# A hybrid decoder step on one NeuronCore: a slot of its own for the last norm's rows, column sums by transposes, and w_o begun row by row

## The chip, the cores and the metric

The kernel runs on one core of a Trainium2 chip. The time is device microseconds of one execution. TensorE (PE in the profile) multiplies matrices, VectorE (DVE), ScalarE (ACT) and GpSimd (POOL) work element by element, and DMA queues on SyncE (SP), ACT and POOL move data. TensorE writes only into PSUM, eight banks of 128 x 512 floats; DVE and ACT read PSUM. Each engine takes its instructions in a fixed order, and an instruction that waits holds up all behind it on its engine or queue.

## The reference, cut to what matters

One layer for a prompt of 2048 tokens and 32 sample tokens (8 sequences of 4), model width 1024, in fp32:

```python
h = rmsnorm(x, n1);  z = h @ w_in
y_a = (rmsnorm(hgrn(z)) * silu(hg)) @ w_up_a      # recurrent branch
y_b = sliding_window_attention(z) @ w_up_b
m = sigmoid(ga) * y_a + sigmoid(gb) * y_b
x = x + m @ w_o
h2 = rmsnorm(x, n2)
x = x + square(relu(h2 @ w_ff1)) @ w_ff2
y = rmsnorm(x, normf_w)
```

where `rmsnorm(x, w) = x * rsqrt(mean(x*x, -1) + 1e-6) * w`. The outputs are y, the new key and value windows and the new recurrent states.

## The kernel before, in words

**Layout and precision.** Activations stand transposed: the 1024 features lie in eight rows of 128 partitions (k = 0 to 7), the tokens along the free axis. Every fp32 product is made of three matmuls of split operands (high x high, high x low, low x high): `split_out` copies to the high part on ACT and subtracts on DVE to get the low part. So each weight block costs a DMA, an ACT cast and a DVE subtraction. Weight tiles come from one ring, `wtile`, of 12 buffers of 128 x 1024.

**Stages.** The 2080 tokens are four blocks b0 to b3 of 512 (b3 holds the 32 sample tokens too, 544 in all, worked on in segments of 288 and 256). Two blocks make a half: half 0 is b0 and b1, half 1 is b2 and b3. Each block runs projections, recurrence, attention, the gates, and then w_o: eight output rows j, two to a weight unit, each a sum over eight rows of m (L1150 to L1163). In half 1 the projections are done for both blocks at once by a Strassen scheme (z). After b3 follow, for each half, FF1 and FF2, both by a Strassen scheme: FF1 by `strassen_T`, whose units first do their products with A11 and A12 and reach S1 to S4 and A22 later; FF2 in seven steps (`steps`), each a product over 16 blocks in four groups g. Steps one to six add into y (`evac`, L1301); y's rows j 0 to 3 of the first token part are whole after step five, all but the second part's rows 0 to 3 after step six, the rest in step seven, which goes by pairs jp of columns with four weight blocks each.

**Norms.** Each norm needs the mean of squares over the features, which lie across partitions. `Norm.add` squares a row on ACT and sums it into `acc` on POOL (L231). `rstd_row` (L200) sums over the partitions with matmuls against a column of 1/1024 (L207, tiles n_), adds epsilon on DVE (L209), raises to -1/2 on POOL (L210), and spreads the result over all partitions by transposes (L215, tiles rb_), copied out by ACT (L216). `Norm.scale` (L237) then multiplies on DVE. The first norm (L428) squares all eight rows and lets the matmuls sum them too.

**Work beside w_o.** During w_o the list `todo` runs pieces of the next work, `per` of them after each j: in b0 the norm of b1's input (tiles xr, na_h), in b1 the two norms of half 1 (zh, na_z; scaled rows are stored to DRAM, hraw, and the first half's are split into hT, which the next projection reads), in b2 a reload, in b3 `ff_sums`, FF1's sums of h2. The norm of w_o's own result (n2, tiles na_fb) is ended later, among the next block's projections (`late`).

**The last norm.** `Fin` (L1270) holds one token part of y: `add(j)` loads the residual row x1 into a `wtile` (on SP), adds it, squares into another `wtile`, and sums on POOL; `end` is the norm, `out(j)` scales and stores. Both parts are handled within step seven, their pieces again in a list `todo`, two after each group.

**What sets the order.** The code gives only priorities. A planner simulates the program with its own estimates of durations and puts on each engine, in turn, the ready instruction that comes first in the code; buffers are given out in the same pass. So moving code moves instructions only as far as that plan lets them, and the plan's estimates can be off.

## Time and profile before

| what | value |
|---|---|
| runs shown | 2982.37, 2985.49, 2986.84 us |
| median | 2985.49 us |
| profiled execution, own time | 2984.1 us |
| its span, first to last instruction | 2982.3 us |
| mean granted clock of TensorE | 0.973 |
| DMA queue of SP and ACT issues (q1) | 334.41 MB, 35.8% of 16 engines' time |
| DMA queue of POOL issues (q0) | 131.41 MB, 12.0% |

Spans and durations in the profile are of one execution. The profile's answers give, for a group of instructions, busy time and the mean duration of one, then the idle time of the engine just before them and what ended it. PE's waits are idle time that the trace puts down to the last semaphore to come. A matmul's recorded duration overlaps with the next one's, so the cost of a matmul is read from a dense stretch and not from its own record.

### The profile page before, as it was taken

What the parts mean: (1) busy time and instruction counts of PE and PEld (TensorE: products, weight loads), DVE (VectorE), ACT (ScalarE), POOL (GpSimd) and SP (SyncE); (2) the same over time, 40 slices, a digit from 0 to 9 for tenths busy, and PEclk for the clock granted to TensorE, in tenths of its full rate; (3) what the DMA queues carried; (4) which work ended last, traced back from release to release, by engine and by line L of the source; (5) the groups of instructions that cost most, each with busy time, mean ns of one, the idle gap of its engine ahead of it and who ended that gap; (6) DMA issues with size and microseconds to landing.
All of it is one profiled execution on the core that took longest, in us unless ns stands there. A gap on an engine that the chain in (4) does not pass through costs nothing.

```text
span 2982.3 us, 50304 instructions
## 1 busy us (share of the span) xinstructions
PE 2823.5 (95%) x20169; PEld 2461.4 (83%) x20169; DVE 1720.7 (58%) x2742; ACT 1131.4 (38%) x2128; POOL 556.0 (19%) x825
## 2 busy tenths in 40 slices
PE   8999999999899999999998999999987999999995
PEld 6778787787799968777897788778866999999994
DVE  3474444754765357436667877654556776644454
ACT  3442334423444444234334333444423333344331
POOL 0100321002510101320133222110023333300002
PEclk9999999999899999999999999999988999999997
DMA  4227642277553423423367544785546444555553
GB/s 136 78 74 251 202 130 67 63 252 229 183 190 101 147 85 119 154 81 101 106 216 236 175 155 156 247 279 197 188 158 199 150 156 142 182 193 190 179 174 123
DMA packets 342970, 480.31 MB, mean 161 GB/s; under 512 B 22208, under 2 KB 223760, under 8 KB 342720
## 3 DMA queue, kind: packets, MB, share of 16 engines
q1 hardware_dynamic: 292080, 334.41, 35.8%
q0 software_dynamic: 40288, 131.41, 12.0%
q10 hardware_dynamic: 10368, 11.28, 1.1%
q8 instruction: 158, 2.59, 0.4%
q14 instruction: 76, 0.62, 0.1%
HBM read 346.20 MB, written 131.83 MB: 160 GB/s over the span
## 4 chain that ended last, share of the span: by engine, by line
PE 76%; DMA 6%; issue 6%; POOL 5%; DVE 4%; ACT 2%; POOLq 0%; SPq 0%; ACTq 0%; DVEq 0%
PE f L1297 6%; PE f L1299 6%; PE f L1298 6%; PE fB_f L248 4%; PE fB_f L250 3%; PE fB_f L249 3%; PE fD_f L250 2%; PE fD_f L248 2%; PE fD_f L249 2%; PE fB_z L248 1%; PE fB_z L250 1%; PE fB_z L249 1%; PE ps_hgb L161 1%; PE ps_hgb L162 1%; PE ps_hgb L163 1%
## 5 line engine op out<-in xcount | busy, mean ns | idle before, releaser
L1297 PE MATMUL f<-f2S,hw2T 128*128 128x264 f32 (+1 forms) x576 | 185.0, 321 | 2.1 <-ACT hw2T L147 2.1
L1299 PE MATMUL f<-f2S,lw2T 128*128 128x264 f32 (+1 forms) x576 | 184.5, 320 | 0.3 <-DVE lw2T L148 0.3
L1298 PE MATMUL f<-f2S,hw2T 128*128 128x264 f32 (+1 forms) x576 | 184.6, 321 | 0.0
L231 POOL TENSOR_TENSOR na_y<-na_y,nq_y 128x512 f32<-128x512 f32 (+2 forms) x35 | 39.2, 1120 | 554.7 <-ACT nq_y L230 553.7
L148 DVE TENSOR_TENSOR lw2T<-lw2T,hw2T 128x1024 fp32r<-128x1024 f32 x64 | 78.1, 1227 | 99.5 <-ACT hw2T L147 98.7
L161 PE MATMUL wob<-m_b,h_wob 128*128 128x512 f32 (+2 forms) x320 | 115.9, 362 | 12.0 <-DVE x_b L1158 5.3
L248 PE MATMUL fB_f<-S,w1T_f 128*128 128x264 f32 (+1 forms) x384 | 123.5, 322 | 3.9 <-ACT c_f L310 3.2
L1297 PE MATMUL f<-f2A,h_w2B 128*128 128x264 f32 (+1 forms) x384 | 122.5, 319 | 0.6 <-ACT c_f L1202 0.6
L249 PE MATMUL fB_f<-S,w1T_f 128*128 128x264 f32 (+1 forms) x384 | 122.6, 320 | 0.0
L250 PE MATMUL fB_f<-S,w1T_f 128*128 128x264 f32 (+1 forms) x384 | 122.6, 320 | 0.0
L1298 PE MATMUL f<-f2A,h_w2B 128*128 128x264 f32 (+1 forms) x384 | 122.3, 319 | 0.0
L1299 PE MATMUL f<-f2A,l_w2B 128*128 128x264 f32 (+1 forms) x384 | 122.2, 318 | 0.0
L1297 PEld LDWEIGHTS f<-f2S,hw2T 128*128 128x128 f32 x576 | 109.0, 189 | 10.1 <-ACT hw2T L147 2.6
L162 PE MATMUL wob<-m_b,h_wob 128*128 128x512 f32 (+2 forms) x320 | 116.0, 362 | 1.1 <-DVE m_b L241 1.1
L147 ACT CAST hw2T<-lw2T 128x1024 fp32r<-128x1024 f32 x64 | 66.9, 1050 | 130.0 <-DMA lw2T<-w_T 129.6
L1299 PEld LDWEIGHTS f<-f2S,lw2T 128*128 128x128 f32 x576 | 108.7, 189 | 8.7 <-DVE lw2T L148 1.0
L163 PE MATMUL wob<-m_b,l_wob 128*128 128x512 f32 (+2 forms) x320 | 115.6, 362 | 0.0
L1298 PEld LDWEIGHTS f<-f2S,hw2T 128*128 128x128 f32 x576 | 109.1, 189 | 7.7
L148 DVE TENSOR_TENSOR f2S<-f2S 128x1024 fp32r<-128x1024 f32 (+1 forms) x64 | 79.1, 1240 | 46.9 <-ACT f2S L147 45.6
L240 ACT CAST w1T_f<-w1r_f 128x512 fp32r<-128x512 f32 x128 | 77.2, 619 | 72.3 <-DVE w1r_f L284 32.3
L241 DVE TENSOR_TENSOR l_w2B<-rw2B,h_w2B 128x1024 fp32r<-128x1024 f32 x48 | 58.7, 1223 | 75.5 <-ACT h_w2B L240 61.6
L241 DVE TENSOR_TENSOR w1T_f<-w1r_f,w1T_f 128x512 fp32r<-128x512 f32 x128 | 87.1, 687 | 25.9 <-ACT w1T_f L240 25.7
(794 smaller groups left out, 9486.3 us busy)
## 6 DMA issues: line engine op xcount, KB each, us to landing
w1r_f<-w_ff SPq DMA_DIRECT2D x64, 512.0 KB
lw2T<-w_T SPq DMA_DIRECT2D x64, 512.0 KB
rw2B<-w_ff SPq DMA_DIRECT2D x48, 512.0 KB
f2S<-u_S SPq DMA_DIRECT2D x32, 528.0 KB
ws<-w_ff SPq DMA_DIRECT2D x32, 512.0 KB
r_wob<-w_o SPq DMA_DIRECT2D x32, 512.0 KB
f2S<-u_S SPq DMA_DIRECT2D x32, 512.0 KB
u_S<-s_f POOLq DMA_DIRECT2D x96, 132.0 KB, 2.4
```

Of the source, the lines that this page charges most:

```text
L148: nc.vector.tensor_tensor(lo, F(lo), F(hi), ALU.subtract)
L161: nc.tensor.matmul(ps[:, 0:n], wh, rh, start=(k == 0), stop=False)
L162: nc.tensor.matmul(ps[:, 0:n], wh, rl, start=False, stop=False)
L163: nc.tensor.matmul(ps[:, 0:n], wl, rh, start=False, stop=(k == nk - 1))
L240: nc.scalar.copy(dh, src)
L241: nc.vector.tensor_tensor(dl, src, F(dh), ALU.subtract)
L248: nc.tensor.matmul(ps, wh, ah, start=(first and k == 0), stop=False, skip_group_check=not first)
L249: nc.tensor.matmul(ps, wh, al, start=False, stop=False, skip_group_check=not first)
L250: nc.tensor.matmul(ps, wl, ah, start=False, stop=(last and k == 3), skip_group_check=not first)
L1297: nc.tensor.matmul(ps, wh, ah, start=first, stop=False, skip_group_check=cont)
L1298: nc.tensor.matmul(ps, wh, al, start=False, stop=False, skip_group_check=cont)
L1299: nc.tensor.matmul(ps, wl, ah, start=False, stop=lastk, skip_group_check=cont)
```

## The change

- `rstd_row`: the accumulated squares are transposed by TensorE, 128 (or 88, 68) tokens at a time, into PSUM, and one DVE reduction per chunk sums over the features; one DVE instruction multiplies by 1/1024 and adds epsilon. The column `ones` is gone. The first norm's eight squared rows are summed on DVE.
- `Norm.add` takes an engine: DVE in b0, for the first of the two norms in b1, and for n2 in b3; POOL otherwise. Of the gate sums of m, row 6 goes to DVE as row 7 did.
- w_o: the first two output rows (n = 0) go row by row of m over both; PSUM tiles come from three rings in turn, not two; evictions and `todo` pieces come after each pair of output rows, one piece after each row. The lists are cut anew: in b0 and b1 a norm's end comes later in the list; in b1 the halves interleave, and hraw is stored two rows at a time on ACT's queue.
- `Fin`: residual rows and squares live in `xo`, slot 6 of the eight-row operand slots, in eight columns that are used in turn; `load` is apart from `add`; the first part's loads and its first four adds move into step six; the sums for the second part's rows 0 to 3 go to DVE, the others stay on POOL. In the last half one piece follows each group.

```diff
-    def rstd_row(dst, sqs, n, tmp, name):
+    def rstd_row(dst, sq, n, tmp, name):
-        ps = tp_ps(f"n_{name}")[0:w, 0:nt]
-        for i in range(nt):
-            for j, sq in enumerate(sqs):
-                nc.tensor.matmul(ps[:, i:i + 1], sq[:, i * w:(i + 1) * w], ones, start=(j == 0), stop=(j == len(sqs) - 1))
         rs = tmp("ns", f"rs_{name}")[0:w, 0:nt]
-        nc.vector.tensor_scalar(rs, ps, EPS, None, ALU.add)
+        for t0, ln in chunks_of(n):
+            ps = tp_ps(f"n_{name}_{t0}")[0:w].rearrange("p (c e) -> p c e", e=P)[:, 0:ln // w]
+            for i in range(ln // w):
+                nc.tensor.transpose(ps[:, i], sq[:, t0 + i * w:t0 + (i + 1) * w], ident)
+            nc.vector.tensor_reduce(rs[:, t0 // w:(t0 + ln) // w], ps, AX.X, ALU.add)
+        nc.vector.tensor_scalar(rs, rs, 1.0 / D, EPS, ALU.mult, ALU.add)
...
-        def add(u, x):
+        def add(u, x, eng=nc.gpsimd):
-                nc.gpsimd.tensor_tensor(u.acc, u.acc, q, ALU.add)
+                eng.tensor_tensor(u.acc, u.acc, q, ALU.add)
...
     for k in range(KD):
         nc.scalar.activation(sq0[:, k], x0[:, k], AF.Square)
+        if k:
+            tt(sq0[:, 0], sq0[:, 0], sq0[:, k], ALU.add)
...
-                (nc.vector if j == KD - 1 else nc.gpsimd).tensor_tensor(o, o, pb[:, j, t0:t0 + n], ALU.add)
+                (nc.vector if j >= KD - 2 else nc.gpsimd).tensor_tensor(o, o, pb[:, j, t0:t0 + n], ALU.add)
...
-            todo += [loads, lambda: [nn.add(xr[:, k]) for k in range(4)], lambda: [nn.add(xr[:, k]) for k in range(4, 8)] + [nn.end()]]
-            todo += [lambda k=k: fin1(k) for k in range(0, KD, 2)]
+            todo += [loads, lambda: [nn.add(xr[:, k], nc.vector) for k in range(4)], lambda: [nn.add(xr[:, k], nc.vector) for k in range(4, 8)],
+                     lambda: None, nn.end, lambda: [fin1(0), fin1(2)], lambda: [fin1(4), fin1(6)]]
...
-                        nc.gpsimd.dma_start(hraw[sb + 1][k * P:(k + 1) * P, o * Tn:(o + 1) * Tn], xr[:, k])
+                        if k % 2:
+                            nc.scalar.dma_start(kmaj(hraw[sb + 1], k - 1, 2, o * Tn, Tn), xr[:, k - 1:k + 1])
+            (ld0, sq0_, end0, fin0), (ld1, sq1_, end1, fin1_) = half
+            todo += [ld0, lambda: sq0_(0), lambda: [sq0_(4), ld1()], lambda: sq1_(0), lambda: [end0(), sq1_(4)], lambda: fin0(0),
+                     lambda: [fin0(4), end1()], lambda: [fin1_(0), fin1_(4)]]
...
+        rings = (sw_ps, mm_ps, hg_ps)
         for n in range(0, KD, 2):
             uo = [unit_rows(w_o, 4 * kh, 4, n * P, 2 * P, f"wo{B}{n}{kh}") for kh in range(2)]
+            ps = [[rings[j % 3](f"wo{B}{j}_{t0}")[:, 0:ln] for (t0, ln) in segs] for j in (n, n + 1)]
+            order = [(k, j, i) for j in range(2) for i in range(len(segs)) for k in range(KD)]
+            for k, j, i in (sorted(order) if n == 0 else order):
...
+                nc.tensor.matmul(p, wh, ah, start=(k == 0), stop=False)
+                nc.tensor.matmul(p, wh, al, start=False, stop=False)
+                nc.tensor.matmul(p, wl, ah, start=False, stop=(k == KD - 1))
+            for j in range(2):
...
+                n2.add(x1[:, n + j], nc.vector if last_b else nc.gpsimd)
+                if todo:
+                    todo.pop(0)()
...
+                def load(f, j):
                     c0 = f.o * Th + f.t0
-                    nc.sync.dma_start(x, x1d[sb][j * P:(j + 1) * P, c0:c0 + f.ln])
+                    nc.sync.dma_start(f.x(f.regs[j]), x1d[sb][j * P:(j + 1) * P, c0:c0 + f.ln])
+                def add(f, j, eng=nc.gpsimd):
+                    x = f.x(f.regs[j])
                     tt(f.y(j), f.y(j), x, ALU.add)
-                    f.n.add(f.y(j))
+                    nc.scalar.activation(x, f.y(j), AF.Square)
+                    if f.acc is None:
+                        f.acc = x
+                    else:
+                        eng.tensor_tensor(f.acc, f.acc, x, ALU.add)
...
+            f0 = Fin(0, 0, Th, {**{j: j for j in range(KD)}, "rb": 1})
+            f1 = [Fin(1, t0, ln, {4: 2, 5: 3, 6: 4, 7: 5, 0: 6, 1: 7, 2: 3, 3: 4, "rb": 5})
...
+                if si == 5:
+                    xo = raw8(6, Th, f"xo{sb}")
+                    todo += [lambda: [f0.load(j) for j in range(4)], lambda: [f0.load(j) for j in range(4, 8)],
+                             lambda: [f0.add(0), f0.add(1)], lambda: [f0.add(2), f0.add(3)]]
...
-                    if not last and si >= 1 and g % 2 and todo:
+                    if todo and (si == 5 or g % 2):
                         todo.pop(0)()
...
+            todo = [lambda j=j: f0.add(j) for j in range(4, KD)]
+            todo = todo[2:] + [each("load", 0, 1)] + todo[:2] + [each("load", 4, 5, 6, 7), none, f0.end, none]
+            outs = [lambda j=j: f0.out(j) for j in range(KD)]
+            todo += [each("add", 4), outs[0], each("add", 5), outs[1], each("add", 6), each("load", 2, 3), outs[2], each("add", 7)] + outs[3:]
...
-                            for _ in range(2):
+                            for _ in range(1 if last else 2):
...
-                        f.add(2 * jp + j)
+                        f.add(2 * jp + j, nc.vector)
```

More of the change, by code (lines that the diff above doesn't have):

```diff
@@ L104, in tile_hybrid_step @@
     n1c, n2c, l0, l1, nfc = cols[:, 0:8], cols[:, 8:16], cols[:, 16:20], cols[:, 20:24], cols[:, 28:36]
-    ones = cp.tile([P, 1], F32, name="ones")
-    nc.gpsimd.memset(ones, 1.0 / D)
     ident = cp.tile([P, P], F32, name="ident")
@@ L431, in tile_hybrid_step @@
         nc.scalar.activation(sq0[:, k], x0[:, k], AF.Square)
+        if k:
+            tt(sq0[:, 0], sq0[:, 0], sq0[:, k], ALU.add)
     rb0 = t2("rb0")
-    rstd_row(rb0, [sq0[:, k] for k in range(KD)], bt, wk_tmp, "first")
+    rstd_row(rb0, sq0[:, 0], bt, wk_tmp, "first")
     for k in range(KD):
@@ L1126, in tile_hybrid_step @@
             z_half = [raw8(4 + g, Tn, f"zh{g}") for g in range(2)]
+            half = []
             for o, xr in enumerate(z_half):
@@ L1233, in y_tmp @@
             def y_tmp(tag, name):
[L1234 to L1236 removed]
+                return fp.tile([P, 8], F32, tag="ns", bufs=2, name=name)
             def w2_blk(o, k0, nk, c0, nc_, name):
@@ L1307, in evac @@
                     tt(o, ps, o, ALU.add)
+            f0 = Fin(0, 0, Th, {**{j: j for j in range(KD)}, "rb": 1})
+            cut = Th // 2 if last else Th
+            f1 = [Fin(1, t0, ln, {4: 2, 5: 3, 6: 4, 7: 5, 0: 6, 1: 7, 2: 3, 3: 4, "rb": 5})
+                  for t0, ln in (((0, cut), (cut, Th - cut)) if last else ((0, Th),))]
+            todo = []
             for si, (ao, wo) in enumerate(steps[:6]):
```

58 lines of the change are left out of this document (24 added, 34 removed).

## The prediction

> **What bounds the kernel now.** I read the page first, then TensorE's waits, then the busy time by stage, then the timelines around TensorE's longest gaps. The waits' columns are total us, times, longest.
>
> ```profile
> PE 2823.5 (95%) x20169; PEld 2461.4 (83%) x20169; DVE 1720.7 (58%) x2742; ACT 1131.4 (38%) x2128; POOL 556.0 (19%) x825
> ```
>
> ```profile
> PE f L1297 <- ACT hw2T L147: 28.4, 3, 18.5
> PE n_y L207 <- POOL na_y L231: 26.8, 4, 14.9
> ...
> PE n_h L207 <- POOL na_h L231: 6.2, 1, 6.2
> ```
>
> TensorE is the bound, so only its waits, and the time that it runs at a lower granted clock, can be won. The large waits belong to norms: to their column sums (n_), or to weights cast behind them (hw2T). The change touches these places, so I cost it by stage. Columns: stretch, length, busy us (count) of PE, PEld, DVE, ACT and POOL, granted clock, DMA share, GB/s.
>
> ```profile
> 5.00:27.30 22.30, 15.70 (x69) 14.93 (x69) 4.22 (x15) 6.50 (x13) 1.04 (x1) 1.00 0.68 247
> 343.50:397.70 54.20, 48.00 (x206) 39.61 (x205) 28.44 (x34) 21.68 (x32) 25.69 (x21) 0.91 0.43 143
> 718.80:781.60 62.80, 52.57 (x229) 42.14 (x228) 24.30 (x33) 25.93 (x40) 36.04 (x35) 0.91 0.58 195
> 1207.80:1259.90 52.10, 47.66 (x194) 37.39 (x193) 23.17 (x26) 16.67 (x21) 18.98 (x17) 0.93 0.41 133
> 1533.10:1592.40 59.30, 52.00 (x385) 50.95 (x385) 40.55 (x63) 22.61 (x34) 23.74 (x34) 0.94 0.78 271
> 2179.10:2264.60 85.50, 52.47 (x217) 42.15 (x215) 41.02 (x52) 25.61 (x34) 32.37 (x32) 0.78 0.55 184
> 2890.60:2970.10 79.50, 53.44 (x405) 51.71 (x403) 37.41 (x63) 18.38 (x32) 21.78 (x22) 0.81 0.40 131
> 2970.10:2982.40 12.30, 1.07 (x9) 0.81 (x9) 4.32 (x11) 0.80 (x2) 1.59 (x2) 0.69 0.26 89
> ```
>
> These are the first norm; the w_o stages of b0 to b3; the seventh step of FF2 for half 0 and half 1; the tail. What the matmuls alone take I read from two undisturbed stretches of FF2 (f's instructions only, PE first):
>
> ```profile
> 2150.00:2200.00 50.00, 50.00 (x222) 41.42 (x221) 8.12 (x13) 0.00 (x0) 1.00 0.55 185
> 2863.00:2890.00 27.00, 27.00 (x225) 27.00 (x225) 6.29 (x18) 0.00 (x0) 1.00 0.52 165
> ```
>
> A 512-wide matmul takes 50.00/222 = 0.225 us, a 264-wide one 27.00/225 = 0.120. By the code the stages of b0, b1, b2 and step seven of half 0 have 4 x 48 = 192 of the first (43.2 us); step seven of half 1 has 384 of the second (46.1); b3 has 384 of mean width 272 (384 x 0.120 x 272/264 = 47.5). The excess over that is all there is to win: 11.0 (b0), 19.6 (b1), 8.9 (b2), 11.8 (b3), 42.3 and 33.4 us.
>
> **The first norm** (gain 7.5). Its column sums stand alone between the last square and the first real matmul:
>
> ```profile
> 10.58 1.15 ACT L431 ACTIVATE sq<-x 128x512 f32<-128x512 f32 x2 [1.46 <-DMA x<-xT]
> 11.26 11.34 PE L207 MATMUL n_first<-ones,sq 128*128 128x1 f32 x52 [1.50 <-ACT sq L431]
> 24.05 1.11 PE L215 MATMUL rb_first<-ident,rs_first 128*128 128x128 f32 x4 [1.45 <-POOL rs_first L210]
> 27.28 0.80 PE L184 MATMUL ps_hib<-h_hib,hT 128*128 128x512 f32 x1 [2.11 <-ACT hT L240]
> ```
>
> Prices of the new operations come from these groups (busy, mean ns):
>
> ```profile
> L1284 DVE TENSOR_TENSOR y<-y,fx_y 128x512 f32<-128x512 f32 x16 | 11.2, 714 | 3.5 <-DMA fx_y<-x1d 3.5
> L879 DVE TENSOR_REDUCE mx_b0c<-W_b 128x8 f32<-128x1024 f32 x4 | 4.8, 1209 | 0.0
> L819 DVE TENSOR_REDUCE mxs<-ss 128x1 f32<-128x160 f32 x2 | 0.6, 321 | 0.1
> L231 POOL TENSOR_TENSOR na_z<-na_z,nq_z 128x528 f32<-128x528 f32 x14 | 18.9, 1350 | 8.3 <-ACT nq_z L230 7.8 <-ACT na_z L227 0.5
> ```
>
> Six of the seven DVE sums run while squares still arrive; the last costs 0.71 us. Four transposes like rb_first's take 1.11. No row sums 512 elements from PSUM: the price lies between 0.32 (160 wide) and 1.21 (1024 wide); I take half of the latter, 0.60, since width sets it. From the end of the column sums, 11.26 + 11.34 = 22.60, to 27.28 all stays, 4.68. So 10.58 + 1.15 + 0.71 + 1.11 + 0.60 + 4.68 = 18.8, plus about 1 for handoffs: the first matmul comes 7.5 us earlier (6 to 8.5).
>
> **b0 and b1** (gains 8 and 10). The sums of squares of b0, and of the first half in b1, go from POOL (1.35) to DVE (0.71), and the norm's end is issued after the third pair of w_o's columns, 6 x 24 x 0.225 = 32.4 us into the stage, where its operand is long ready. The 6.2 us of b0 go, and b1's 4.7 with its second half's wait, each with the half-rate stretch behind it. b0 keeps two sets of transposes, 2 x 1.11 us: 8 of its 11.0 (4 to 9). In b1 something else becomes late:
>
> ```profile
> 742.45 1.92 PE L207 MATMUL n_z<-ones,na_z 128*88 128x1 f32 x12 [4.72 <-POOL na_z L231]
> ```
>
> ```profile
> 757.62 0.64 ACT L240 CAST hT<-zh 128x528 fp32r<-128x528 f32 x1 [1.90 <-DVE zh L237]
> ```
>
> Now the norm begins 742.45 - 718.8 = 23.7 us into the stage and hT is whole 758.26 - 742.45 = 15.8 us later. After the change that is 32.4 + 15.8 = 48 us, but w_o ends at about 46, and the next GEMM reads all eight rows of hT for its first output tile. The new wait is 0 to 6 us; I take 10 of 19.6 (6 to 15). The eight single stores of hraw per half, on POOL, become four double ones on ACT, issued at 1.86/4 = 0.47 us each by the row below, 8 x 0.47 = 3.8 us, behind scalings that the casts there wait for too. ACT is idle 37 of b1's 62.8 us, which hides it; without that cover it is 3.8 us.
>
> ```profile
> 0.73 1.86 ACTq L429 DMA_DIRECT2D x<-xT  x4
> ```
>
> **b2 and b3** (gains 7 and 5). In b2, w_o waits for m's last two rows; in b3 an eviction on DVE is late, queued behind a split of FF1's weights whose DMA is late:
>
> ```profile
> 1215.66 0.50 PE L161 MATMUL wob<-m_b,h_wob 128*128 128x512 f32 x1 [2.77 <-ACT m_b L240]
> ...
> 1218.35 0.80 PE L161 MATMUL wob<-m_b,h_wob 128*128 128x512 f32 x1 [1.11 <-ACT m_b L240]
> ```
>
> ```profile
> 1579.22 0.69 DVE L241 TENSOR_TENSOR w1B_f<-w1r_f,w1B_f 128x512 fp32r<-128x512 f32 x1 [3.32 <-ACT w1B_f L240]
> ```
>
> ```profile
> 1580.30 0.58 PE L161 MATMUL wob<-m_b,h_wob 128*128 128x256 f32 x1 [4.96 <-DVE x_b L1158]
> ```
>
> Row by row over two columns, row 6 is needed 36 x 0.225 = 8.1 us after the stage's start and row 7 at 9.5, against 1215.66 - 1207.8 = 7.9 and 10.6 today; with row 6 summed on DVE both come about 1.5 us earlier. The waits go, with a half-rate stretch: 7 of 8.9. In b3 three PSUM rings give TensorE one column more before it needs that eviction (48 x 0.124 = 5.9 us, over the 4.96). But DVE, busy 40.55 us there, gets seven 544-wide sums, 7 x 0.75 = 5.3: 45.8 us against 47.5 of matmuls, so I take 5 of 11.8 (0 to 10).
>
> **FF2's seventh step** (gains 29 and 26). Half 0 waits 14.9 us at its last norm. In half 1 the second group of weights is issued on SP behind outputs and residual rows, as their buffers are of one ring:
>
> ```profile
> 2258.08 1.87 PE L207 MATMUL n_y<-ones,na_y 128*128 128x1 f32 x8 [14.92 <-POOL na_y L231]
> ```
>
> ```profile
> 2925.46 5.57 SPq L1293 DMA_DIRECT2D out_yT<-y  x8
> 2931.12 5.89 SPq L1283 DMA_DIRECT2D fx_y<-x1d  x9
> 2937.57 2.02 SPq L1250 DMA_DIRECT2D lw2T<-w_T  x4
> ```
>
> ```profile
> 2942.47 0.59 PE L1297 MATMUL f<-f2A,hw2T 128*128 128x264 f32 x1 [18.55 <-ACT hw2T L147]
> ```
>
> Residual rows and squares leave the ring, so the 12 buffers hold the first group's eight tiles and half of the second. The first norm's eight residual loads move a step earlier on SP, ahead of weights that wait for buffers anyway (0.41 us each, 3.3 in all), and four adds with them. Half 0: 43.2, two norms' transposes (about 3; four sets of at most 1.11), and DVE's 41.0 us of work changed by -4 x 0.71 + 4 x 0.71 + 2 x 0.60: 42.2 us, nearly as long as the matmuls. So I leave 10 us of waits: 56.5, a gain of 29 (17 if the 14.9 us stay and half as much again is lost to the lower clock, 42.3 - 3 - 22.4; 38 if nothing waits). Half 1: 46.1 + 3 + 4.4 for its last two weight tiles, whose buffers come free 7 us before their use: 53.5, a gain of 26 (29 if they are in time; 14 if they come 15 us late).
>
> The slot of the residual rows holds half 0's last reciprocal root until its last scaling, and FF1 of half 1 loads S2 into that slot, on POOL's in-order queue ahead of other operands:
>
> ```profile
> L248 PE MATMUL fB_f<-S,w1T_f x13: 280/284/287, 2299.5 to 2310.0; 128*128 128x264 f32 x13
> ```
>
> ```profile
> L497 POOL DMA_DIRECT2D S<-dS x6: 722/722/738, 2235.3 to 2252.1; - x6
> ...
> L148 DVE TENSOR_TENSOR S<-S x6: 1249/1257/1258, 2242.1 to 2261.2; 128x1056 fp32r<-128x1056 f32 x6
> ```
>
> Today the S loads start 8 us before step seven's last matmul (2258.08 - 14.92 = 2243.2) and serve at 2299.5. After the change S2's start about 14 us behind that matmul (the tail, the same work on 264 columns, takes 12.3), need about 10 to land and be split (2242.1 + 1.3 - 2235.3 = 8.1 for one half of an operand), and are used after ten units, 10 x 24 x 0.120 = 28.8 us in. Later operands queue behind: 0 to 8 us, I take 2. The four h2 norms gain a DVE leg (0.60 and its queue), 1 us each. The tail trades POOL's last sum for a sum over transposes: 0, within 0.5.
>
> **Sum.** 7.5 + 8 + 10 + 7 + 5 + 29 + 26 - 2 - 4 = 86.5 us. The profiled execution took 2984.1, so 2897.6; the median of the runs is 1.4 above it, so 2899 us.
>
> In FF2's two stages the granted clock is 0.78 and 0.81, against 1.00 in the undisturbed stretches. [...]
>
> **The rivals.**
>
> *FF2 keeps its waits* (17 in 100). If the new loads stand on SP ahead of the second weight group just as the old ones did, half 0 gains 17 and half 1 gains 3 to 14: about 30 less, 2930 us. For it: out_yT of half 1 stays on SP. Against: the ring no longer couples them.
>
> *The norms were no bound* (7 in 100): in-order waits reappear at the next instruction, and only the first norm, b2 and b3 win: 7.5 + 7 + 5 - 4 = 15.5, so 2970 us. For it: b3's wait came from a DMA, not from a norm.
>
> *Slower: DVE's queue carries the norm* (6 in 100). Each of the 13 norms (first, h, four h2, two z, five in FF2) now passes DVE twice, for sums and for the transposes' sum, with TensorE committed in order behind. A split waiting for its DMA held DVE in b3, and TensorE lost 4.96 us and, at that stage's mean clock of 0.94, 0.06 x 59.3 = 3.6 us more: 8.5. If that happens at all 13 norms, 111 us are lost against 86.5 gained: 3010 us. It decides from 86.5/8.5, more than ten norms. For it: DVE near full in b3 and in half 0. Against: 28.44/54.20 = 52% busy in b0, 39% in b1. [...]
>
> **How the numbers follow.** Forecast 66 in 100 (2868 to 2922 by the bounds above), FF2's waits 17, norms no bound 7, slower 6, nothing measurable 4. The range 2868 to 2945 leaves out the last three and the ends. Changes under 0.2% can't be told from none here. Faster 0.89, same 0.04, slower 0.07.
>
> **What would show it.** Right: the first ps_hib matmul near 20 us; no wait over 2 us at n_h, n_z or n_y; lw2T's second group cast before step seven's middle; b0 to b3 at about 46, 53, 45, 54 us; granted clock above 0.95 in step seven. Wrong: waits of PE on DVE at the new sums, on hT after b1, or on S operands 30 us into half 1's FF1.

## The result and the profile after

The changed kernel takes 2945.31 us (median; 2942.32 to 2949.18), the kernel before 2986.16 beside it. The ratio is 0.9864, with an interval from 0.9845 to 0.9883: 40.6 us faster where 86.5 had been forecast, and 0.3 us above the high end of the predicted range. The profiled execution took 2947.49 us, its span 2945.7, at a mean granted clock of 0.981.

The page of the kernel after, busy time by engine:

```profile
PE 2799.7 (95%) x20053; PEld 2440.9 (83%) x20053; DVE 1762.8 (60%) x2802; ACT 1130.2 (38%) x2128; POOL 505.4 (17%) x772
```

DVE has taken 42 us of work, POOL lost 51. TensorE's waits in the kernel after (total us, times, longest):

```profile
PE n_first L206 <- DVE sq L432: 15.3, 1, 15.3
PE rb_z L214 <- POOL rs_z L209: 12.2, 2, 11.0
PE fB_f L247 <- ACT c_f L309: 11.8, 7, 4.0
PE n_y L206 <- POOL xo L1300: 9.0, 2, 5.8
PE fC_f L247 <- DVE p_f L324: 8.6, 2, 6.8
PE fB_f L247 <- DVE x_b L1168: 7.5, 1, 7.5
PE fC_z L247 <- ACT w1B_z L239: 5.4, 1, 5.4
...
PE n_y L206 <- DVE xo L1300: 4.4, 2, 2.4
PE rb_y L214 <- POOL rs_y L209: 4.1, 3, 1.8
PE rb_h L214 <- POOL rs_h L209: 3.8, 1, 3.8
```

The long waits of before (18.5 at FF2's weights, 14.9 at the last norm) are gone. (The 15.3 us at n_first are the time to TensorE's first instruction, not a wait within the work.) In their place stand shorter ones, most of them where no wait was before: behind the norm's root (rb_z, rb_h), and at the first products of the next GEMM (fC_z, fB_f, fC_f). Busy time by stage, after, from b0's w_o to step seven of half 1; columns as in the prediction:

```profile
337.30:388.50 51.20, 47.44 (x202) 38.83 (x201) 32.21 (x39) 21.60 (x32) 13.95 (x14) 0.93 0.50 159
705.60:764.40 58.80, 47.77 (x210) 39.21 (x209) 29.92 (x36) 23.75 (x37) 24.46 (x21) 0.88 0.55 189
805.90:1018.60 212.70, 206.00 (x1657) 203.47 (x1656) 113.63 (x199) 92.92 (x194) 12.81 (x22) 0.99 0.43 133
1205.10:1249.90 44.80, 44.33 (x194) 35.90 (x193) 24.01 (x27) 17.15 (x21) 16.41 (x16) 1.00 0.49 157
1525.40:1586.30 60.90, 49.67 (x385) 48.63 (x385) 42.43 (x72) 23.04 (x35) 16.86 (x29) 0.98 0.79 269
2174.30:2227.00 52.70, 46.73 (x203) 37.87 (x202) 40.28 (x46) 18.85 (x26) 23.04 (x23) 0.94 0.59 193
2227.00:2583.90 356.90, 336.74 (x2660) 332.89 (x2660) 256.05 (x528) 128.88 (x267) 125.63 (x230) 0.97 0.48 159
2870.40:2933.30 62.90, 54.08 (x404) 51.78 (x402) 42.22 (x69) 15.89 (x28) 16.74 (x13) 0.95 0.39 128
```

The third row is the z stage (from its first product to the next projections), the seventh the handover (from half 0's last f matmul to half 1's first, with FF1 of half 1 inside). The prediction did not show these two of before:

```profile
823.00:1026.80 203.80, 203.59 (x1657) 201.84 (x1656) 110.84 (x194) 90.18 (x191) 12.29 (x21) 1.00 0.42 135
2243.20:2603.50 360.30, 334.23 (x2665) 330.62 (x2666) 257.36 (x532) 132.33 (x273) 130.17 (x233) 0.96 0.49 160
```

Subtracting the stages' starts and ends in the two profiles gives where the 36.6 us between the two spans came from (forecast in the last column; half 0's 29 split at its last f, less 2 for the operands). Each stage is read from one execution, and the four of the changed kernel spread over 6.9 us, so a difference of a few us in one stage says something only where other kernels repeat it:

| from one landmark to the next | saved, us | forecast |
|---|---|---|
| start to b0's w_o (the first norm) | 6.2 | 7.5 |
| b0's w_o | 3.0 | 8 |
| b0's w_o to b1's | 4.0 | 0 |
| b1's w_o | 4.0 | 10 |
| b1's w_o to b2's (the z stage alone: -8.9) | -14.5 | 0 |
| b2's w_o | 7.3 | 7 |
| b2's w_o to b3's | -2.3 | 0 |
| b3's w_o to FF1's first product | -1.6 | 5 |
| FF1 and FF2 of half 0 to step seven | -1.3 | -4 (h2 norms) |
| step seven of half 0, to its last f | 11.4 | 7.7 |
| handover | 3.4 | 19.3 |
| FF2 of half 1 to step seven | 0.6 | 0 |
| step seven of half 1 | 16.6 | 26 |
| tail | -0.1 | 0 |

Two losses stand out: the handover gave 3.4 of 19.3, and all that had been won by the end of b1's w_o (17.2 us) was down to 2.7 at the start of b2's. The z loss repeats: z takes 203.6 to 205.4 us in the kernels without the w_o part (before, and only_fin and only_norm below) and 207.9 to 217.4 in all that have it. Almost all of the other 5.6 us stand behind z, in b2's projections, recurrence and attention, at a clock of 0.98 against 1.00; no run was aimed at them.

### The profile page after: what moved, and what is told of

Read it like the earlier page. It is cut to its first block, busy times and chain, and to the rows that moved or that the text cites. A ratio compares the mean times of both kernels' runs of the same rounds, so it can differ in the third digit from the quotient of the medians.

```text
span 2945.7 us, 50018 instructions
## 1 busy us (share of the span) xinstructions
PE 2799.7 (95%) x20053; PEld 2440.9 (83%) x20053; DVE 1762.8 (60%) x2802; ACT 1130.2 (38%) x2128; POOL 505.4 (17%) x772
## 4 chain that ended last, share of the span: by engine, by line
PE 75%; issue 7%; DMA 6%; DVE 5%; POOL 4%; ACT 2%; SPq 0%; POOLq 0%; ACTq 0%; DVEq 0%
PE f L1315 7%; PE f L1313 7%; PE f L1314 7%; PE fB_f L247 3%; PE fB_f L249 3%; PE fB_f L248 3%; PE fD_f L249 1%; PE fD_f L247 1%; PE fD_f L248 1%; PE ps_hgb L159 1%; PE ps_hgb L160 1%; PE fB_z L247 1%; PE ps_hgb L161 1%; PE fB_z L249 1%; PE fB_z L248 1%
## 5 line engine op out<-in xcount | busy, mean ns | idle before, releaser
L1300 POOL TENSOR_TENSOR xo<-xo 128x512 f32<-128x512 f32 (+2 forms) x25 | 34.4, 1379 | 503.1 <-ACT xo L1296 489.6
```

## The experiments

Gains are against the kernel before, from the ratio and its interval. The theory (A in most expectations) is that the parts work as costed, and that the rest went into new waits at the next instruction in order. Its rivals are named with each run.

**One part alone, and one part left out.** The transposes and DVE's sum with the first norm; the w_o part with the old statistics; the last norm's slot with the old statistics; and the change without the new statistics.

```diff
# only_norm: before, and
+            for i in range(ln // w):
+                nc.tensor.transpose(ps[:, i], sq[:, t0 + i * w:t0 + (i + 1) * w], ident)
+            nc.vector.tensor_reduce(rs[:, t0 // w:(t0 + ln) // w], ps, AX.X, ALU.add)
...
+        if k:
+            tt(sq0[:, 0], sq0[:, 0], sq0[:, k], ALU.add)
```

> The kernel before, with the new statistics alone: transposes and one DVE sum in all 13 norms, the first norm's squares summed on DVE. Everything else (sums on POOL, order of w_o, slots of FF2) is as before. Theory A (what the trace after shows at the first norm, 5.4 us, is all that the transposes win, since at the other norms TensorE waits for the sum that comes before them): 4 to 8 us faster than before. Theory B (the second trip over DVE delays a norm by 1 to 2 us each, and this is where the forecast's gain was lost): 10 to 20 us slower than before.

```diff
# only_wo: before, and
+            for k, j, i in (sorted(order) if n == 0 else order):
...
+                n2.add(x1[:, n + j], nc.vector if last_b else nc.gpsimd)
# with the rings, the lists, the engines of the sums and the double hraw stores of the change
```

> The kernel before, with the w_o part alone: two rows of m summed on DVE, the first pair of output rows row by row, three PSUM rings, the lists cut anew, the sums of squares on DVE in b0, b1's first half and b3, hraw stored on ACT's queue. Norms and FF2 are as before. Theory A (the losses between b1 and b3, 9 us in the z stage and 7 us at FF1's start, come from this part's own order): 5 to 15 us faster than before. Theory B (those losses come from the transposes' trip over DVE; this part alone wins what the forecast gave it): 22 to 30 us faster.

```diff
# only_fin: before, and
+                    xo = raw8(6, Th, f"xo{sb}")
# with load, add and the lists of Fin as in the change
```

> The kernel before, with the last norm's part alone: residual rows and squares in slot 6, loads and four adds in step six. Norms are made as before. Theory A (half 0's gain is handed on to FF1 of half 1, which cannot evacuate before the last norm's rows are stored; half 1 wins about 18 us): 25 to 36 us faster than before. Theory B (the forecast's 29 + 26): 50 us or more faster. Theory C (FF2 keeps its waits): 17 us or less.

```diff
# no_norm: only_wo and only_fin together
```

> The kernel before, with the w_o part and the last norm's part together, and the norms' statistics as before (column sums by matmuls, the first norm's too). Alone, the three parts won 16.7, 14.3 and 33.7 us by their ratios, 64.7 in sum, where the whole change won 40.6. Theory A (the statistics' second trip over DVE makes a wait where w_o has become dense: 3.8 us at rb_h in b0, with a half-rate stretch, where the w_o part alone has none): this kernel is 35 to 48 us faster than before, within 8 us of after; b0's w_o stage takes 45 us as in the w_o part alone, not 51. Theory B (the parts do not touch each other, the missing 24 us are lost elsewhere, whichever norm is used): 20 to 26 us faster than before. Theory C (the last norm and the w_o part add up): 48 us faster or more.

| kernel | median, us | ratio (interval) | gain, us |
|---|---|---|---|
| only_norm | 2970.55 | 0.9944 (0.9927 to 0.9961) | 16.7 |
| only_wo | 2972.67 | 0.9952 (0.9938 to 0.9967) | 14.3 |
| only_fin | 2954.07 | 0.9887 (0.9872 to 0.9903) | 33.7 |
| no_norm | 2939.70 | 0.9833 (0.9809 to 0.9857) | 49.8 |
| after | 2945.31 | 0.9864 (0.9845 to 0.9883) | 40.6 |

The parts won 64.7 us one by one and 40.6 together. w_o and the last norm add up (48.0 against 49.8); the statistics won 16.7 alone and nothing on top of the other two (40.6, from 34.9 to 46.3, against 49.8, from 42.7 to 57.0). So these edits don't add up, and a sum of stages, each costed by itself, can't show that. Against the expectations, only_wo and only_fin came out as A had them; only_norm above A's 4 to 8 and far from B's loss. Beside the first norm it won 4 to 5 us in b1, and its handover took 350.3 us against 360.3, which neither theory had. b0's stage in only_wo:

```profile
342.70:387.80 45.10, 45.10 (x205) 37.24 (x204) 29.39 (x35) 20.91 (x30) 12.79 (x14) 1.00 0.53 173
```

With the old column sums, b0's w_o runs without a wait of TensorE in 45 us, at a clock of 1.00, in no_norm too (45.2); with the new ones it takes 51.2. That looked like a price of the transposes themselves, and was tested again at the end (best_sums).

**The first norm.** After, in order of time:

```profile
9.65 0.35 DVE L120 CAST cu<-scratch 128x368 uint8<-128x368 f32 x1 [2.90 <-DMA scratch<-c_msk]
9.92 3.88 DVE L432 TENSOR_TENSOR sq<-sq 128x512 f32<-128x512 f32 x5
10.51 1.15 ACT L430 ACTIVATE sq<-x 128x512 f32<-128x512 f32 x2 [1.38 <-DMA x<-xT]
...
15.30 1.12 PE L206 MATMUL n_first<-ident,sq 128*128 128x128 f32 x4 [15.30 <-DVE sq L432]
16.51 0.68 DVE L207 TENSOR_REDUCE rs_first<-n_first 128x4 f32<-128x512 f32 x1
...
21.89 0.79 PE L182 MATMUL ps_hib<-h_hib,hT 128*128 128x512 f32 x1 [2.11 <-ACT hT L239]
```

The last square ends at 11.66, but DVE's sums at 15.3: it stood 2.90 us for the mask's transfer before it began them, and had seven left. cu_late moves that cast behind the norm in the code.

```diff
-    nc.vector.tensor_copy(cu, cu_f)
...
+    nc.vector.tensor_copy(cu, cu_f)    # behind the first norm
```

> The kernel after, with one cast of constants on DVE (scratch to cu) moved behind the first norm. In the trace after it stands ahead of the sums of squares and waits for its DMA until 9.65 us. Theory A (it holds the seven sums): the first transposes come 2 to 3 us earlier than 15.30 us, and the total is 2 to 3 us less. Theory B (the rows of x and the squares are late themselves): less than 1 us.

2940.45 us, 0.9842 (0.9818 to 0.9865). It did not test what it was meant to: the planner left the cast where it was (at 9.83 us, after 3.00 us of waiting for the same transfer), and the transposes' time with it. So the 4.9 us below the kernel after aren't from there, and the intervals overlap. Of the 8.7 us between the two profiled spans 7.7 stand in FF1 and FF2 of half 0 (588.0 and 580.3 us), which the edit doesn't touch: that much can differ between nearly equal kernels. The cause of the 2.9 us is read from the trace only.

**b0.** The norm's end in the kernel after:

```profile
372.86 1.28 POOL L230 TENSOR_TENSOR na_fb<-na_fb,nq_fb 128x512 f32<-128x512 f32 x1
373.61 1.61 DVE L240 TENSOR_TENSOR l_hib<-r_hib,h_hib 128x1024 fp32r<-128x1024 f32 x1 [0.81 <-ACT h_hib L239]
374.08 2.05 POOL L209 TENSOR_TENSOR rs_h<-rs_h,negh 128x4 f32<-128x4 f32 x1
376.19 1.11 PE L214 MATMUL rb_h<-ident,rs_h 128*128 128x128 f32 x4 [3.76 <-POOL rs_h L209]
```

The wait at the sums (n_h) has become a wait at the root's spread (rb_h): POOL first finished a sum of another norm, and its root then took 2.05 us, against 1.05 before. Only 1.0 of the 3.76 us is thus the slower root; the rest is the links before it. best3, whose edits are told below, also ends this norm one piece earlier; the wait went back to the sums and the stage took 51.1 us, as before that edit (51.2), where 45 to 48 had been expected:

```profile
364.89 1.09 PE L206 MATMUL n_h<-ident,na_h 128*128 128x128 f32 x4 [3.67 <-DVE na_h L230]
```

**b1 and z.** The one wait that grew most, after:

```profile
748.96 1.30 POOL L230 TENSOR_TENSOR na_z<-na_z,nq_z 128x528 f32<-128x528 f32 x1 [0.75 <-ACT nq_z L229]
750.22 2.34 POOL L209 TENSOR_TENSOR rs_z<-rs_z,negh 88x6 f32<-88x6 f32 x1
752.61 1.14 PE L214 MATMUL rb_z<-ident,rs_z 88*128 88x88 f32 x6 [11.03 <-POOL rs_z L209]
```

POOL, which still does the second half's sums, does these as their squares arrive, the last as the first row shows, and takes up the first half's root only behind them. Two ways out: end the first norm before the second begins, or move those sums to DVE.

```diff
# b1_early: after, and
-            todo += [ld0, lambda: sq0_(0), lambda: [sq0_(4), ld1()], lambda: sq1_(0), lambda: [end0(), sq1_(4)], lambda: fin0(0),
-                     lambda: [fin0(4), end1()], lambda: [fin1_(0), fin1_(4)]]
+            todo += [ld0, lambda: sq0_(0), lambda: [sq0_(4), ld1()], end0, lambda: [fin0(0), fin0(4)], lambda: sq1_(0),
+                     lambda: [sq1_(4), end1()], lambda: [fin1_(0), fin1_(4)]]
# b1_dve: after, and
-                        nn.add(xr[:, k], nc.gpsimd if o else nc.vector)
+                        nn.add(xr[:, k], nc.vector)
```

> The kernel after, with the list of b1 cut so that the first half's norm ends, and its rows are scaled and split, before the second half's sums on POOL begin. Theory A (the root on POOL stands behind the second half's sums, and this makes the 11.0 us wait at rb_z): the wait under 5 us, 5 to 12 us faster than after. Theory B (the z stage is bound by its own chain, the sums zS and their loads): the wait goes but the next projections start within 3 us of where they do after, total within 3 us.

> The kernel after, with the sums of squares of b1's second half on DVE as well. Theory A (POOL's queue of sums holds the root of the first half by 3.6 us, from the end of DVE's 746.61 to POOL's 750.22): 3 to 6 us faster than after. Theory B (DVE is what the stage lacks): 0 to 5 us slower.

b1_early 2939.42 us, 0.9832 (0.9806 to 0.9857); b1_dve 2944.01, 0.9856 (0.9833 to 0.9879). The intervals of both overlap that of the kernel after, so the stages are read and not the totals. The wait at rb_z in w_o goes in part (b1_dve: 5.6 us are left, so POOL's sums were about half of it) or nearly whole (b1_early: 1.5 us there, 1.9 at n_z before it, and 4.9 at n_z of the second half, behind w_o). In b1_early, b1's w_o and then z:

```profile
706.70:755.20 48.50, 45.08 (x205) 36.94 (x204) 30.98 (x42) 20.99 (x32) 13.38 (x13) 1.00 0.71 241
802.20:1019.60 217.40, 208.27 (x1658) 205.42 (x1657) 122.38 (x213) 96.49 (x201) 13.37 (x23) 0.98 0.42 134
```

w_o went from 58.8 to 48.5 us, and z from 212.7 to 217.4: the next projections begin at 1019.6, against 1018.6. TensorE came sooner to a point that did not move: 5.5 us of the 10.3 were already lost between w_o and z, where it waits for the second half's sums, and 4.7 in z. What that point is shows in ACT's order after (the last row is TensorE's):

```profile
798.31 1.17 ACT L239 CAST zS<-zh 128x528 fp32r<-128x528 f32 x2 [8.13 <-DMA h2d<-x_b]
...
817.83 1.07 ACT L145 CAST zS<-zS 128x1056 fp32r<-128x1056 f32 x1 [6.43 <-DMA zS<-zS]
...
819.48 0.59 PE L247 MATMUL fC_z<-hT,w1B_z 128*128 128x264 f32 x1 [5.37 <-ACT w1B_z L239]
```

ACT's cast of z's operand sums waits 8.13 us for the stores of b1's n2 result (h2d). The operand S4 then goes through DRAM and back, and ACT waits for it 6.43 us, with a weight cast in order behind it, for which TensorE waits. That cast of S4 starts at 817.8 here, at 818.8 in b1_early and at 819.7 in b1_n2, below, however early w_o ended. So one more run took the n2 sums of b1 from POOL too, to bring n2's end, and with it the h2d stores, forward:

```diff
# b1_n2: b1_early, and
-                n2.add(x1[:, n + j], nc.vector if last_b else nc.gpsimd)
+                n2.add(x1[:, n + j], nc.vector if last_b or bi == 1 else nc.gpsimd)
```

> The kernel after, with b1's list cut as in the run b1_early, and the sums of squares of w_o's own result in b1 on DVE in place of POOL. In after and in b1_early the first projections of half 1's z stage start earlier than before, but its end does not move. Theory A (the z stage's operand S3 lies in slot 6, where w_o's result waits to be scaled and stored by the norm of b1, and that norm waits for POOL's sums behind those of the next norms): the stores of h2d end 5 to 10 us earlier than the 798 us of after, the z stage ends (b2's first projections) at 1012 or earlier in place of 1019, total 5 to 10 us below b1_early. Theory B (DVE, 77% busy from 775 to 835 us, is the bound there): the z stage ends at 1017 or later.

2926.63 us, 0.9802 (0.9781 to 0.9824): 59.1 us faster than before. z in b1_n2, and ACT there:

```profile
799.20:1009.60 210.40, 205.63 (x1658) 203.50 (x1657) 121.14 (x211) 95.98 (x201) 13.37 (x23) 0.99 0.43 138
```

```profile
819.68 1.07 ACT L145 CAST zS<-zS 128x1056 fp32r<-128x1056 f32 x1 [1.14 <-DMA zS<-zS]
```

The next projections begin at 1009.6, 9 us earlier, which is what A expected; but not by its path. The first h2d store is issued at 788.9 us, against 788.3 after, and S4 lands no sooner. What changed is ACT's order: no wait of it for the store is left in the record, and 1.14 us for S4 in place of 6.43. Why the plan came out so isn't settled. That the loss in z was weights queued behind ACT's waits is read from these rows, and no run took that away alone; only_norm has both waits of ACT (8.5 and 4.2 us) with a z of 205.4 us, so the waits cost only if a weight that TensorE needs stands behind them. The edit's effect is not the 18.7 us between the two medians either: of the 22.0 us between the profiled spans, 9.0 are won by the next projections, and 2.6 more up to b2's w_o, 4.1 between the w_o of b2 and b3 and 5.1 in FF1 and FF2 of half 0, where the code is the same. Of the other kernels with this edit, best1 to best3 below reach the next projections at 1010.4 to 1013.5 us, but best_sums at 1017.1; those with the w_o part and without the edit reach them at 1014.9 to 1023.0.

**b3.** Its stage ends with a wait of 7.5 us at FF1's first product on x_b, DVE's last evictions. Rival: the seven n2 sums that the change gave DVE here hold them.

```diff
# b3_pool: after, and
-                n2.add(x1[:, n + j], nc.vector if last_b else nc.gpsimd)
+                n2.add(x1[:, n + j])
```

> The kernel after, with the sums of squares of w_o's own result in b3 back on POOL. Theory A (the sums on DVE alternate with the evictions and hold up the last four, so that FF1's first unit waits 7.5 us): 4 to 9 us faster than after, the wait of fB_f for x_b under 3 us. Theory B (the splits of FF1's weights, not the sums, hold the evictions): within 2 us of after, the wait stays. Theory C (the forecast's reason for the move, that POOL would be late at the norm): slower than after by 2 to 6 us.

2944.81 us, 0.9852 (0.983 to 0.9873), and the wait in b3_pool:

```profile
PE fB_f L247 <- DVE x_b L1168: 7.2, 1, 7.2
```

Not the sums, then. By the timeline the evictions alternate with subtractions of FF1's weights on DVE, as they did before; three rings only moved the wait from the eighth column to the next GEMM.

**The handover.** After:

```profile
2232.72 0.62 ACT L239 CAST w1B_f<-w1r_f 128x512 fp32r<-128x512 f32 x1 [4.68 <-DMA w1r_f<-w_ff]
...
2234.72 0.59 PE L247 MATMUL fB_f<-A,w1B_f 128*128 128x264 f32 x1 [4.83 <-DVE y L1323]
...
2247.35 5.39 DVE L1307 SCALAR_TENSOR_TENSOR y<-y,cols,xo 128x512 f32<-128x512 f32 x8 [1.15 <-ACT xo L215]
...
2257.60 0.59 PE L247 MATMUL fC_f<-A,w1B_f 128*128 128x264 f32 x1 [6.81 <-DVE p_f L324]
```

TensorE is through with half 0 at 2227.0. It waits first for half 0's last eviction (y) on DVE, which stands behind the split of a weight whose DMA is late. Then, 30 us after half 0's end, it waits for p_f, FF1's own partial sums, whose copies and additions stand in order behind the last norm's work on ACT and DVE and behind FF1's operands. Three suspects, one run each: half 0's stores still hold the buffer under p_f (y_swap); the five late operands are loaded ahead of the first weights (s_late: their loads go behind the first ten units, on SP); the residual rows' slot is handed to an operand that is needed early (s_slot: in half 1 slot 6 goes to S4, the last used).

```diff
# y_swap: after, and (order of y's tiles in memory)
+            for o, j in [(0, 7)] + [(1, j) for j in range(5)] + [(0, j) for j in range(7)] + [(1, j) for j in range(5, KD)]:
# s_late: after, and
+            if sb == 0:
+                while loads:
+                    op_load(*loads.pop(0))
...
+                       pre=lambda: [op_load(*a, q=nc.sync) for a in loads])
# s_slot: s_late, and
-            for nm, slot in zip(("S2", "S1", "S3", "A22", "S4"), (2, 3, 6, 4, 5) if sb == 0 else (6, 4, 5, 2, 3)):
+            for nm, slot in zip(("S2", "S1", "S3", "A22", "S4"), (2, 3, 6, 4, 5) if sb == 0 else (4, 5, 2, 3, 6)):
# no_s4 (its products with S4 read S1, so the result is not the layer's): s_slot, and
+                if sb and nm == "S4":
+                    ff_ops[nm] = ff_ops["S1"]
+                    continue
```

> The kernel after, with only the places of y's sixteen tiles in SBUF changed, so that the tiles that FF1 of half 1 evacuates into first lie over the rows of the first token part, which are stored 45 us earlier, and no longer over rows 3, 2, 1, 0 of the second part. Theory A (the store of the last norm's rows is what holds FF1's evacuation, 6.5 us of idle ACT and 6.8 us of TensorE with a half-rate stretch behind it): 5 to 10 us faster than after, no wait of ACT at p_f for out_yT. Theory B (ACT's and DVE's order holds it: the copy of the norm's root and eight scalings stand ahead in any case): within 2 us of after.

> The kernel after, with the loads of S1 to S4 and A22 for FF1 of half 1 moved from POOL's queue to SP's and in the code behind the first ten units, so that FF1's first three weight units are loaded before them. Theory A (5.3 MB of operands, loaded while the last norm runs, make FF1's first weights late, and their splits stand ahead of the last eviction on DVE and of its square on ACT): the last eviction of half 0 less than 3 us after its matmul (7.0 in after), FF1 of half 1 8 to 15 us shorter than the 357 us of after. Theory B (the weights wait for free buffers, not for the DMA engines): within 3 us. Theory C (the operands then come late themselves): PE waits at S operands, slower than after.

> The kernel s_late, with the slots of FF1's operands in half 1 changed so that S4, which is used last, lies in slot 6 in place of S2, which is used first. In s_late ACT waits 8.8 us for S2, whose slot is held by the last norm's root until its last scaling, with five evacuations of FF1 behind it. Theory A (that wait holds TensorE's 8.5 us at fC_f): the wait under 4 us, 4 to 10 us faster than s_late. Theory B (DVE's eight scalings and five sums of weights hold it, as in y_swap): the wait stays at 5 to 8 us, within 3 us of s_late.

> The kernel s_slot without the load and the split of S4 for FF1 of half 1: its products read S1 in place of S4, so nothing of FF1 waits for slot 6 any more (y of half 1 is not the layer's). Two loads of 0.53 MB, two casts and two subtractions are left out. Theory A (the cast of S4 on ACT, which waits 9.6 us for its load and has five evacuations of FF1 behind it, holds TensorE's 9.0 us at fC_f): the wait falls under 4 us, the stretch from half 0's last FF2 matmul to half 1's first is 342 us or less in place of 348.2. Theory B (DVE's eight scalings and the sums of the weights hold it in any case, as in y_swap): a wait of 5 to 7 us stays, the stretch is 345 us or more.

| kernel | median, us | ratio (interval) | handover, us | wait at fC_f, us |
|---|---|---|---|---|
| after | 2945.31 | 0.9864 (0.9845 to 0.9883) | 356.9 | 6.8 |
| y_swap | 2948.33 | 0.9873 (0.9855 to 0.9890) | 356.2 | 6.8 |
| s_late | 2936.26 | 0.9847 (0.9801 to 0.9894) | 351.3 | 8.5 |
| s_slot | 2934.93 | 0.9826 (0.9797 to 0.9856) | 348.2 | 9.0 |
| no_s4 | 2932.73 | 0.9814 (0.9791 to 0.9837) | 348.6 | 3.8 |

y_swap took ACT's wait for the stores away and left TensorE's as it was: that theory fell. In s_late TensorE's wait for the last eviction fell from 4.8 to 0.5 us, and the handover by 5.6 of the 8 to 15 us that A expected. Loads and slot together gave 8.7 us of the handover. s_slot's A, though, that the wait at fC_f falls under 4 us, did not come true. In s_slot it is again the residual rows' slot that ACT waits for, now with S4, five copies of p_f behind it:

```profile
2242.61 1.07 ACT L145 CAST S<-S 128x1056 fp32r<-128x1056 f32 x1 [9.57 <-DMA S<-dS]
2243.59 1.50 ACT L309 COPY p_f<-fB_f 128x264 f32<-128x264 f32 x5
```

no_s4 takes that operand out. Its waits and its handover:

```profile
PE fC_f L247 <- DVE p_f L324: 3.8, 1, 3.8
```

```profile
2220.30:2568.90 348.60, 334.52 (x2662) 330.55 (x2661) 253.94 (x526) 127.00 (x266) 124.26 (x226) 0.98 0.50 166
```

The wait at p_f fell from 9.0 to 3.8 and the handover didn't move (348.2, 348.6): the wait for the norm's root (rb_y) ahead of it grew from 2.3 to 3.5 us, and the copies wait 4 us for the stores of y. That loads and slot matter shows in other kernels too: the handover takes 355.0 to 359.4 us in the eight that have them as in the change (after, y_swap, and those of b1, b3, f0_dve and cu_late), 345.9 to 352.3 in the six that have s_slot's (s_slot, no_s4 and the four below), 7.7 us less in the mean. So about 8 us of the missing 15.9 are shown to come from the operands' loads and their slot. The rest is read as the last norm's chain in front of FF1 on three engines; which link of it decides stays open.

**Step seven's sums.** In both halves the norm of the first token part waits for POOL's sums (n_y on POOL, 5.8 and 3.2 us). f0_dve gives all of them to DVE.

```diff
# f0_dve: after, and
-            todo = [lambda j=j: f0.add(j) for j in range(4, KD)]
+            todo = [lambda j=j: f0.add(j, nc.vector) for j in range(4, KD)]
# and the same for the four adds in step six
```

> The kernel after, with all sums of squares of the last norm's first token part on DVE in place of POOL, in both halves. Theory A (TensorE's waits of 5.8 us in half 0 and 3.2 us in half 1 at n_y are POOL's slow sums, 1.6 us each): waits under 2 us, with the half-rate stretches 6 to 10 us faster than after. Theory B (the squares come late, behind casts on ACT that wait for their DMA): 0 to 3 us.

2942.18 us, 0.9848 (0.9824 to 0.9872). Waits in half 0's step seven, f0_dve:

```profile
PE rb_y L214 <- POOL rs_y L209: 3.4, 1, 3.4
PE n_y L206 <- DVE xo L1300: 1.8, 1, 1.8
```

The wait at POOL's sums went, and in half 0 the wait for the root, the next link of the same norm, took 3.4 us in its place. Step seven of half 1 took 59.2 us against 62.9, and 58.6 to 59.8 in the four kernels below, which have this edit too. The total shows no change clear of noise.

**All that helped, together.** best1: s_slot, b1_early's list, f0_dve, and of the n2 sums those of b1 on DVE and b3's back on POOL. best2: s_slot, b1_n2, f0_dve and cu_late. best3: s_slot, b1_n2, f0_dve and b0's norm one piece earlier. best_sums: best1 with the old column sums everywhere but in the first norm.

```diff
# best3, beside those edits
-                     lambda: None, nn.end, lambda: [fin1(0), fin1(2)], lambda: [fin1(4), fin1(6)]]
+                     nn.end, lambda: None, lambda: [fin1(0), fin1(2)], lambda: [fin1(4), fin1(6)]]
# best_sums, beside best1
-            rstd_row(u.acc, u.acc, u.n, u.tmp, u.N)
+            rstd_ones(u.acc, [u.acc], u.n, u.tmp, u.N)
```

> The kernel after, with the edits of b1_n2, f0_dve, s_late and s_slot together, and the sums of squares of w_o in b3 back on POOL. If each term shown so far adds up: 59.1 us in the profile of b1_n2, 4.5 more in half 1's seventh step from f0_dve, 5.6 from s_late, 2 from b3: about 2914 us. If the planner's new order takes some back, as it did with the three parts: 2920 to 2927 us.

> As best1, but with the sums of squares of w_o in b3 on DVE as in after, and with the cast of constants behind the first norm as in cu_late. It tells whether those two do anything beside the others: no more than 3 us from best1 if not.

> As best1, but with the sums of squares of w_o in b3 on DVE as in after, and with b0's norm ended one piece earlier. Theory A (in after and best1 TensorE's order leaves eight matmuls, 1.8 us, between the transposes of b0's norm and those of its root, and the root on POOL stands behind a sum of w_o's squares, which makes the 3.8 to 4.3 us wait at rb_h): with twelve matmuls between them, at a place where the sums are further back, b0's w_o stage takes 45 to 48 us in place of 50.3 in best1. Theory B (POOL's queue delays it wherever it ends): 50 us or more. The total: 2915 to 2922 us.

> The kernel best1, with the statistics of all norms but the first made as before (column sums by matmuls against the column of 1/1024). Theory A (where w_o is dense the transposes cost more than they save: no_norm, with the statistics as before throughout, is 9 us below after, though the first norm loses 5 us in it): 6 to 14 us faster than best1, b0's w_o stage 45 us in place of 50. Theory B (the order that the planner happens to make explains it): within 4 us of best1.

best1 2920.67 us, 0.9773 (0.9747 to 0.9798); best2 2923.65, 0.9784 (0.9758 to 0.9810); best3 2918.53, 0.9767 (0.9744 to 0.9791); best_sums 2922.00, 0.9781 (0.9756 to 0.9807). The four can't be told apart, and all beat both kernels: 22 to 27 us faster than after by their medians. For best1, 2914 us had been expected if the terms add up and 2920 to 2927 if the new order takes some back, as it did. best_sums bears on the question left from no_norm: with the rest in place, old and new sums take the same time within the noise, and b0's w_o takes 49.0 us with the old ones against 50.4, not 45. So the 9 us between no_norm and the change, if they are real (the intervals overlap), don't look like a price of the transposes as such. That they come from the order that the plan made of them is what is left, and is argued, not shown.

## Why the prediction was right and wrong

- **Direction and the large waits: right.** The 14.9 and the 18.5 us went, and the part with the new slot won 33.7 us alone. The rival "FF2 keeps its waits" fell. That the total came within 0.3 us of the range is luck: the range reached so far because of that rival, and the losses arose elsewhere.
- **The first norm: right, mis-sized.** The first matmul came at 21.89, 5.4 us earlier, not 7.5. The term "the last costs 0.71 us" measured 15.24 - 11.66 = 3.6 from the end of the last square, since DVE waited for an unrelated transfer. The sum over the transposes took 0.68, against an estimate of 0.60.
- **b2: right.** 7.3 us against 7, and its clock rose from 0.93 to 1.00, as the waits at m's last rows went, and with them the stretch at half rate (1216.8 to 1223.7 us in the kernel before).
- **b0: the step that failed is "its operand is long ready. The 6.2 us of b0 go".** It priced the wait at the sums and not the links behind it; a wait of 3.76 us at the root's spread took its place, with 5.8 us at half rate behind it. 3.0 us instead of 8.
- **b1: the same step, and the place of the new wait was wrong.** It was expected on hT after w_o (0 to 6 us); it came within w_o, at rb_z, 11.03 us, about half of it because the second half's sums stayed on POOL ahead of the first half's root.
- **Between the stages: the step that failed is that the sum has no term there,** as if TensorE could use whatever time w_o wins. Between b1's and b2's w_o 14.5 us were lost, 8.9 of them in z.
- **b3: the step "three PSUM rings give TensorE one column more" was true and worth nothing.** TensorE passed the place and waited 7.5 us at the next GEMM for the same evictions. The mechanism of the rival "the norms were no bound" (in-order waits reappear at the next instruction) thus shows in b0, b1, b3 and the handover; its time doesn't, since FF2 won and b3, which it counted among the winners, lost 1.6 us.
- **Half 0: the term "0 to 8 us, I take 2" for the S operands was mis-sized, and its path was another.** s_slot showed 8.7 for loads and slot. TensorE did not wait for the operands themselves: their loads and casts made it wait for y's last eviction (4.8 us) and for p_f (6.8). The 19.3 us forecast for the handover shrank to 3.4. The 10 us of waits allowed within step seven were more than enough: it took 52.7 us against 56.5 (the terms 43.2 + 3 + 10 give 56.2).
- **Half 1: 16.6 instead of 26.** The term for the last two weight tiles (4.4) held: TensorE's waits for w_T's tiles there are 2.9 us. The step that failed allowed no wait at the norms: n_y and rb_y took 5.4 us in that stage, and at its clock of 0.95 another 0.05 x 62.9 = 3.1 went, together 8.5 of the 9.4 missing.
- **The h2 norms and the tail** can't be told apart from their surroundings; the tail is unchanged, as forecast.
- **The slower rival** fell: of the norms only the first and two last ones (4.4 us together) wait for DVE's sums in the kernel after. For POOL's roots TensorE waited 20 us (rb_z 12.2, rb_y 4.1, rb_h 3.8).
- **The range** can't be redone: the lower bounds of the terms add up to 42 us and the upper ones to 112.5, that is 2943 and 2873 us, where the prediction has 2922 and 2868.

Of the signs that the prediction named, b2's time and the first norm's were near. That no wait over 2 us is left at n_y failed (5.8, 3.2), as did the times of b0 (51.2 for 46), b1 (58.8 for 53) and b3 (60.9 for 54); step seven's clock came to 0.94 and 0.95, not above.

## What to carry to other kernels

When a wait is taken away in a kernel whose engines run in a fixed order, price what follows: read which instruction TensorE reaches next and when its operands arrive in absolute time, because a stage that ends earlier only arrives earlier at a point that may not have moved (in b1_early w_o won 10 us, and the next projections came no sooner). A chain such as sum, root, spread has to be moved to a free engine link by link until none is late; one link alone moves the wait to the next. Effects of edits in a planned program don't add up (64.7 alone, 40.6 together), so a bundle is worth taking apart again after it has been timed.

## What the runs showed of the hardware

**The root on POOL took up to 2.7 us longer where DVE was in an operation on two SBUF inputs as it began.** The root on 128 x 4 values took 2.05 us in b0, where a subtraction of 1.61 us had begun 0.47 us before it (above), and 3.75 us in s_late:

```profile
2233.23 3.75 POOL L209 TENSOR_TENSOR rs_y<-rs_y,negh 128x4 f32<-128x4 f32 x1 [22.68 <-DVE rs_y L208]
2233.66 2.42 DVE L146 TENSOR_TENSOR A<-A 128x1056 fp32r<-128x1056 f32 x2
```

Here a shorter subtraction (0.68 us) had begun 0.17 us before the root, and these two followed it; the root ends 0.9 us after them (2233.66 + 2.42 = 2236.08; 2233.23 + 3.75 = 2236.98). In the first norm of before the subtraction began after the root, and the root took 1.04 us, as long as roots of this shape with no such operation beside them (1.04 to 1.05 us in the kernels before and after):

```profile
22.96 1.04 POOL L210 TENSOR_TENSOR rs_first<-rs_first,negh 128x4 f32<-128x4 f32 x1 [18.22 <-DVE lbw L445]
...
23.08 1.21 DVE L241 TENSOR_TENSOR l_hib<-r_hib,h_hib 128x1024 fp32r<-128x1024 f32 x1
```

The traces of before and after hold 26 roots of norms. The 11 that began while DVE ran such an operation, with both inputs in SBUF, took 0.14 to 1.60 us longer than the same shape undisturbed. The other 15 agree with it within 0.012 us; among them are two beside which such an operation began later (at 22.96 us in before, 1593.51 in after) and one that found an operation running with an input in PSUM (1.35 us, at 769.56 in after). What makes the root longer the rows don't show. In the kernel after, six of the 13 roots were lengthened so, by 5.3 us in all; the rest of TensorE's 20 us at the roots comes from the links before them.

**TensorE ran at half rate for 5 to 6 us after two of its new waits.** After the 3.76 us wait in b0 and around the 11.03 us wait in b1, after:

```profile
375.20:382.00 6.80, 5.81 (x16) 4.75 (x17) 4.06 (x8) 3.39 (x5) 0.94 (x1) 0.50 0.00 0
743.80:757.50 13.70, 4.89 (x16) 4.02 (x17) 7.60 (x10) 5.49 (x10) 9.02 (x8) 0.50 0.18 57
```

TensorE resumed at 376.2 and 752.6 and ran at a granted clock of 0.50 to 382.0 and 757.5, its 512-wide matmuls 0.43 us apart where they then came 0.23 us apart. Of these 5.8 and 4.9 us about half, 2.9 and 2.4 us, was lost, an estimate from the clock. The prediction counted such stretches with the waits that go, and had no term for one behind a wait that takes their place.
